# Queries, keys and values of the stick-breaking and undilated heads kept in DRAM, and sixteen seven-product pairs per layer

## The chip, the cores and the metric

The kernel runs on one core of a Trainium2 chip. The core has a matrix engine (TensorE, PE in the profile), a vector engine (VectorE, DVE), an engine for activations and copies (ScalarE, ACT), a general one (GpSimd, POOL) and SyncE (SP), which here issues nearly all DMA transfers. Each engine takes its own instructions in order. The metric is the device time of one execution in microseconds; less is better.

## The reference, cut to what matters

Two layers over 1024 tokens of width 1024, all in float32. Per layer:

```python
h = rmsnorm(x, norm1[l])
qa, ka, va, qb, kb, vb, gate_pre = split(h @ w_in[l])
o_a = dilated_mixture(qa, ka, va)            # 12 heads of 64: 4 undilated, 4 with dilation 4, 4 with 16
o_b = stick_breaking_attention(qb, kb, vb)   # 4 heads of 64
g_a, g_b = split(sigmoid(gate_pre + b_gate[l]))
x = x + (g_a * (o_a @ w_br[:256]) + g_b * (o_b @ w_br[256:])) @ w_o[l]
a, v = split(rmsnorm(x, norm2[l]) @ w_up[l])
x = x + (gelu(causal_conv(a)) * v) @ w_down[l]
```

and a last rmsnorm. The undilated heads see a window of 128 keys, the dilated ones every 4th or 16th key. Stick-breaking weighs key s for query t by `sigmoid(z_ts)` times the product of `1 - sigmoid(z_tj)` over all j between s and t.

## The kernel before, in words

Every float32 operand is split in two parts of a shorter type, `hi` and `lo` (`split`, L132: a ScalarE cast and a VectorE subtraction), and a product is three matmuls: hi by hi, hi by lo, lo by hi. A **plain** product of 128 columns of weights with 512 tokens is 8 x 3 matmuls of 128x512 (`product`, L167). A **seven-product pair** (`pair`, L1012) computes two such blocks of columns over all 1024 tokens as a 2 by 2 block product with seven instead of eight block products. It needs sums of blocks of `h` (`block_sums`, L951, kept as `t_hi`, `t_lo`; POOL, VectorE and ScalarE make them from `h_sum`) and sums of blocks of the weights, made anew for every pair on POOL and VectorE.

The mixer of a layer (`mixer`, L1169) runs in this order. `head` (L581) makes the stick-breaking values and the first two heads' keys and queries. Then `attend` (L328) walks a list of attention items: 16 of stick-breaking (`stick_item`, four heads by four blocks of 256 queries), 4 undilated or near ones (`near_item`, one per head), 16 dilated or far ones (`far_item`, which serve both dilations). An item has score steps and, per block of keys, a `turn` (transposes) and an `apply` (products with the values). After each such step `Dense.advance` (L301) adds the item's rate to an account and issues that many steps of **dense work** from a list: a step is six 512-wide matmuls, or their like. TensorE's order is exactly the order in which this Python is written out (`manual_schedule` for PE); the other engines and SP are ordered by a planner, by priority and by when its model thinks an instruction is ready.

Dense work before: `dense.main` holds the second stick-breaking pair's keys and queries, the undilated values and the two undilated pairs' keys and queries as plain units, and six seven-product pairs for the dilated heads; `dense.plain` holds 8 plain gates (`PLAIN`), `dense.seven` 4 gate pairs. `choose` (L225) takes seven-product pairs from `main` only when no plain gate is left. `until` (L309) issues dense steps until a name is done; `aside` (L245) issues one piece of the block sums at a time. What an attention item waits for by name (`first` in `attend`) is a count of dense steps, not a semaphore: `LEAD` is the number of steps between the order of a fetch and the name that lets the item in.

Keys, queries and values of the dilated heads go to DRAM (`tk`, `tv`) with tokens regrouped and come back per item (`fetch_kq`, L800; `fetch_v`, L805). Those of the stick-breaking and undilated heads stay in SBUF (`R["kb"]`, `R["qb"]`, `R["vb"]` and so on). When an item list ends, `join` (L905) merges the dilated and the undilated outputs with factors made by `factors` (L880), and the branch products `br_ps` follow.

Buffers go by tags with a fixed number of slots: `xa` has 4 (values, the fetched keys and queries, the near output `on`, later x), `e8` has 6 (keys, queries, `stay`, and the block sums), `ql` 2 (the low parts of queries, then the raw weights of a pair), `ps`, `s`, `t`, `o` 2 PSUM banks each.

Of the kernel before, what the change touches and what calls it, by code (L numbers as in the profile page):

```python
# [12 lines left out]
ALU = mybir.AluOpType  # L13
# [29 lines left out]
RATE = (0.68, 0.85, 0.72, 0.62)  # L43
RATE_B = (0.9, 1.6, 0.75, 1.1, 0.65, 0.9, 0.6, 0.3)
PLAIN = 8
# [12 lines left out]
def trunk_kernel(ctx, tc, x, norm1, w_in, b_gate, w_br, w_o, norm2, w_up, conv_w, conv_b, w_down, norm_f, out, depth=None, probe=None):  # L58
# [57 lines left out]
    tv = [dr.tile([2, 4, P, 2, 256], F32, name=f"tv{i}") for i in range(2)]  # L116
    dn = [dr.tile([4, T], F32, name=f"dn{i}") for i in range(2)]
# [14 lines left out]
    def split(hi, lo, src, turn=None):  # L132


        one = act.copy(hi, src)  # L135
        if turn == "is":
            LAST["act"] = one.ins.name
        elif turn == "waits" and LAST:
            tc.add_manual_dep(one.ins, LAST["act"], NO_SYNC, reason="in turn")
        two = dve.tensor_tensor(lo, src, f32(hi), ALU.subtract)  # L140
        if turn == "is":
            LAST["dve"] = two.ins.name
        return two
# [68 lines left out]
    class Dense:  # L212
# [4 lines left out]
        def __init__(self):  # L217
# [5 lines left out]
            self.scored = self.applied = self.kq = self.v = 0  # L223

# [24 lines left out]
        def fetch(self):  # L249
# [4 lines left out]

            while self.kq < self.scored + 2 and there(self.kq):
# [72 lines left out]
    def attend(dense, items):  # L328
# [4 lines left out]
        for i, (name, first, rest, rate, make) in enumerate(items):  # L333
# [37 lines left out]
            for j, f in enumerate(seq):  # L371
                if nxt and j >= at:
# [133 lines left out]
    def new_v(name):  # L506
        return [sb.tile([P, 4, 4, P], F32R, tag="xa", bufs=4, name=name) for _ in range(2)]

    def values(key, l, off):
        w = weights(w_in[l][:, off : off + 256], 256)  # L510
        yield
        vt = R[key] = new_v(key)
        yield from values_part(vt, w, range(4))

    def values_part(vt, w, ms):
        for m in ms:
# [15 lines left out]
            dve.tensor_tensor(vv[:, :, :, 64:128], ov, f32(vv[:, :, :, 0:64]), ALU.subtract)  # L532
            yield


    def keys_half(kt, w, n):
        o = bank("ps", "k_ps")
        yield from product(o, [(w[k], h_part(n, k)) for k in range(KD)])
        ka, kb = (kt[:, i, n * HF : (n + 1) * HF] for i in range(2))
        act.copy(ka[0:64], o[0:64])  # L540
        act.copy(kb[64:128], o[64:128])
        dve.tensor_tensor(ka[64:128], o[0:64], f32(ka[0:64]), ALU.subtract)
        dve.tensor_tensor(kb[0:64], o[64:128], f32(kb[64:128]), ALU.subtract)
        yield

    def queries_half(q, w, n, scale):
        qt, ql = q
        o = bank("ps", "q_ps")
        yield from product(o, [(w[k], h_part(n, k)) for k in range(KD)])
        qa, qb, la, lb = (a[:, i, n * HF : (n + 1) * HF] for a in (qt, ql) for i in range(2))  # L550
        for q2, src in ((qa, o[0:64]), (qb, o[64:128])):
            act.mul(q2[0:64], src, scale)
            act.mul(q2[64:128], src, scale)
        dve.scalar_tensor_tensor(la[0:64], o[0:64], scale, f32(qa[0:64]), ALU.mult, ALU.subtract)
        dve.scalar_tensor_tensor(lb[64:128], o[64:128], scale, f32(qb[64:128]), ALU.mult, ALU.subtract)
        yield

    def new_q():


        qt, ql = big("qt", F32R), sb.tile([P, 2, T], F32R, tag="ql", bufs=2, name="ql")
        for rows, i in ((slice(64, 128), 0), (slice(0, 64), 1)):
            zeros_ = pool.memset(f32(ql[rows, i, :]), 0.0)
            tc.add_manual_dep(zeros_.ins, LAST["pool"], NO_SYNC, reason="in turn")
        return qt, ql

    def keys(key, l, off):
        w = weights(w_in[l][:, off : off + P], P)
        yield
        kt = R[key] = big("kt", F32R)  # L570
        for n in range(2):
            yield from keys_half(kt, w, n)

    def queries(key, l, off, scale):
        w = weights(w_in[l][:, off : off + P], P)
        yield
        q = R[key] = new_q()
        for n in range(2):
            yield from queries_half(q, w, n, scale)

    def head(l):  # L581
# [11 lines left out]
        vt = R["vb"] = new_v("vb")  # L593
        kt = R["kb", 0] = big("kt", F32R)
        if l:
            q = R["qb", 0] = new_q()
            yield from values_part(vt, wv, range(2))
        else:
            yield from values_part(vt, wv, range(1))
            wk, wq = others()  # L600
            q = R["qb", 0] = new_q()
            yield from values_part(vt, wv, range(1, 2))
        for n in range(2):
            yield from keys_half(kt, wk, n)
            yield from queries_half(q, wq, n, SCALE)
# [27 lines left out]
    def stick_item(pr, s, qp):  # L633
        if "ob" not in R:
            R["ob"] = big("ob")
        q, k, vt, ob = R["qb", pr], R["kb", pr], R["vb"], R["ob"]
        hd = 2 * pr + s
        rows, st, shared = {}, {}, {}

        def score(a):  # L640
# [3 lines left out]
            if a == 0:  # L644
                st[0] = big("stay")
            sv = st[0][:, a, :]
            for c0 in range(0, L, 512):
                w = min(512, L - c0)
                z = bank("s", "z")
                scores(z[:, :w], *(t[:, s, i * P : i * P + P] for t in q), k[:, s, c0 : c0 + w])  # L650
# [6 lines left out]
            for c1 in range(L, 0, -512):  # L657
                SCANS.append((bt, sv, max(0, c1 - 512), c1, L, pr == 1 and qp == 2 and s == 0))
            if L <= 512:
                scans()  # L660

# [27 lines left out]
        def apply(kb):  # L689
# [4 lines left out]
            for j in range(2):  # L694
                c = P if last and j else 0
                for p in (0, 1):
                    pe.matmul(
                        o[:, c:256],
                        vt[(kb + j) // 4][:, (kb + j) % 4, hd, :],
# [4 lines left out]
                    )  # L704
            if last:
                fold(ob[64 * s : 64 * s + 64, pr, qp * 256 : (qp + 1) * 256], o)
                if (pr, s, qp) == (1, 1, 3):
                    nc.sync.dma_start(obd, ob)
# [5 lines left out]
    def near_item(pr, s):  # L714
# [1319 lines left out]
```

## Time and profile before

| | us |
|---|---|
| median of the runs | 2662.72 (2661.96 to 2663.26, 3 runs) |
| span of the profiled execution | 2660.2 |
| TensorE busy in it | 2647.5 |
| VectorE busy | 2036.5 |
| ScalarE busy | 1349.6 |
| POOL busy | 647.1 |

The median is 2.5 us above the span; the span runs from the first to the last instruction. The granted TensorE clock is full throughout. The first layer's mixer lies at 0 to some 600 us, its feed-forward part up to 1310, the second layer behind it. In rows of instruction groups the columns are line, engine, operation, output and inputs with shapes, count, then busy time and mean nanoseconds of one, then the engine's idle time ahead of them and what ended it. In rows of a timeline they are start and duration in microseconds. In rows of a stretch they are the stretch, its length, then busy time and count of each engine (PE, PEld, DVE, ACT, POOL), the granted clock, the DMA engines' busy share and GB/s. In rows of waits they are the sum, the number and the longest. In rows of one tile the three numbers are the shortest, median and longest duration in nanoseconds. In rows of DMA issues they are the count, the size of one and the median time to landing.

### The profile page before, as it was taken

The page shows a single profiled execution, that of the slowest core. Times are in us where ns is not written, and L with a number is a line of the kernel's source. Part 1 is how long each engine was busy: PE and PEld are TensorE (multiplying, and loading weights), DVE is VectorE, ACT ScalarE, POOL GpSimd, SP SyncE. Part 2 cuts the span into 40 slices and gives each one's busy share as a digit, 9 for nine tenths or more (in the row PEclk, how much of TensorE's full clock was granted, in tenths as well). Part 3 has the DMA queues.
Part 4 walks back from the last instruction along what each step waited for, and adds up shares of the span by engine and source line. Part 5 has one row for each costly group of instructions (what it writes and reads, how often), then busy time and mean ns, then how long its engine had stood idle before and what let it go on. Part 6 is the DMA issues. An engine that isn't in the chain of part 4 may idle for free.

```text
span 2660.2 us, 36616 instructions
## 1 busy us (share of the span) xinstructions
PE 2647.5 (100%) x13084; PEld 2227.1 (84%) x13084; DVE 2036.5 (77%) x3087; ACT 1349.6 (51%) x2490; POOL 647.1 (24%) x473
## 2 busy tenths in 40 slices
PE   9999999999999999999999999999999999999999
PEld 8988888888888888888889888888888888888888
DVE  5877856685888888897658777566958888898865
ACT  6556645474545555432445565455645455554225
POOL 2003211121233344321210051110321343343200
PEclk9999999999999999999999999999999999999999
DMA  5212178673243544688411122785632544446963
GB/s 183 63 53 84 50 196 246 203 263 102 76 150 138 172 143 158 231 310 321 151 40 40 48 84 85 200 263 182 240 97 71 179 138 153 148 168 246 341 242 118
DMA packets 360195, 424.19 MB, mean 159 GB/s; under 512 B 20693, under 2 KB 289357, under 8 KB 357965
## 3 DMA queue, kind: packets, MB, share of 16 engines
q1 hardware_dynamic: 359996, 421.85, 47.8%
q8 instruction: 103, 1.69, 0.3%
q14 instruction: 80, 0.65, 0.1%
q10 hardware_dynamic: 16, 0.00, 0.0%
HBM read 278.07 MB, written 143.72 MB: 159 GB/s over the span
## 4 chain that ended last, share of the span: by engine, by line
PE 91%; DVE 6%; issue 1%; ACT 1%; DMA 1%; POOL 0%; SPq 0%; DVEq 0%; ACTq 0%
PE u_a L945 5%; PE u_a L947 5%; PE u_a L946 5%; PE d_ps L1662 5%; PE d_ps L1664 4%; PE d_ps L1663 4%; PE i_a L945 3%; PE u_c L945 3%; PE u_c L947 3%; PE u_c L946 3%; PE i_a L947 3%; PE i_a L946 3%; PE o_ps L172 2%; PE o_ps L174 2%; PE o_ps L173 2%; PE g_ps L172 2%
## 5 line engine op out<-in xcount | busy, mean ns | idle before, releaser
L140 DVE TENSOR_TENSOR w_lo<-up_a,w_hi 128x512 fp32r<-128x512 f32 x240 | 237.6, 997 | 20.5 <-ACT w_hi L135 20.5
L135 ACT CAST w_hi<-up_a 128x512 fp32r<-128x512 f32 x240 | 149.4, 622 | 183.6 <-PE u_a L946 49.5
L1670 DVE TENSOR_TENSOR x<-x,d_ps 128x512 f32<-128x512 f32 (+1 forms) x228 | 152.0, 672 | 76.8 <-PE d_ps L1664 75.6
L1401 POOL TENSOR_TENSOR cv<-cv 128x512 f32<-128x512 f32 x88 | 132.3, 1515 | 249.3 <-DVE cv L1396 139.4
L140 DVE TENSOR_TENSOR g<-cv,g 128x512 fp32r<-128x512 f32 x154 | 152.1, 988 | 5.2 <-ACT g L135 2.7
L140 DVE TENSOR_TENSOR w_lo<-w_raw,w_hi 128x512 fp32r<-128x512 f32 x144 | 106.4, 741 | 54.9 <-ACT w_hi L135 54.5
L135 ACT CAST w_hi<-w_raw 128x512 fp32r<-128x512 f32 x144 | 89.2, 621 | 105.0 <-PE o_ps L173 50.4
L135 ACT CAST w_hi<-in_a 128x512 fp32r<-128x512 f32 x120 | 74.4, 620 | 114.3 <-PE i_a L946 41.9
L1662 PE MATMUL d_ps<-gd_in,w_hi 128*128 128x512 f32 (+1 forms) x340 | 130.3, 383 | 1.4 <-ACT w_hi L135 0.6
L1664 PE MATMUL d_ps<-gd_in,w_lo 128*128 128x512 f32 (+1 forms) x340 | 129.8, 382 | 0.0
L1663 PE MATMUL d_ps<-gd_in,w_hi 128*128 128x512 f32 (+1 forms) x340 | 129.7, 382 | 0.0
L140 DVE TENSOR_TENSOR w_lo<-in_a,w_hi 128x512 fp32r<-128x512 f32 x120 | 88.6, 738 | 51.0 <-ACT w_hi L135 49.4
L945 PE MATMUL u_a<-hh,w_hi 128*128 128x512 f32 x320 | 124.7, 390 | 0.8 <-DVE u L1552 0.8
L946 PE MATMUL u_a<-hl,w_hi 128*128 128x512 f32 x320 | 124.5, 389 | 0.0
L947 PE MATMUL u_a<-hh,w_lo 128*128 128x512 f32 x320 | 124.5, 389 | 0.0
L947 PE MATMUL u_a<-t_hi,w_lo 128*128 128x512 f32 x320 | 124.5, 389 | 0.0
L945 PE MATMUL u_a<-t_hi,w_hi 128*128 128x512 f32 x320 | 124.5, 389 | 0.0
L946 PE MATMUL u_a<-t_lo,w_hi 128*128 128x512 f32 x320 | 124.5, 389 | 0.0
L1034 POOL TENSOR_TENSOR u<-in_a 128x512 f32<-128x512 f32 x20 | 28.8, 1439 | 369.5 <-DMA in_a<-in_w_in_dram 142.5
L135 ACT CAST g<-cv 128x512 fp32r<-128x512 f32 x154 | 94.9, 617 | 41.2 <-POOL cv L1401 30.0
L669 DVE TENSOR_TENSOR_SCAN stay<-stay,zero 128x512 f32<-128x512 f32 (+2 forms) x96 | 93.5, 974 | 28.0 <-ACT stay L655 27.4
L1662 PE MATMUL d_ps<-gd_in,wd 128*128 128x512 f32 (+1 forms) x292 | 113.9, 390 | 0.0
(412 smaller groups left out, 8694.2 us busy)
## 6 DMA issues: line engine op xcount, KB each, us to landing
gd<-g SPq DMA_DIRECT2D x154, 512.0 KB, 3.5
gd_in<-gd SPq DMA_DIRECT2D x154, 512.0 KB, 5.9
up_a<-in_w_up_dram SPq DMA_DIRECT2D x80, 512.0 KB, 5.3
t_kq<-tk SPq DMA_DIRECT2D x32, 768.0 KB, 5.6
wd_raw<-in_w_down_dram SPq DMA_DIRECT2D x22, 1024.0 KB, 12.6
w_raw<-in_w_in_dram SPq DMA_DIRECT2D x80, 256.0 KB, 3.0
in_a<-in_w_in_dram SPq DMA_DIRECT2D x40, 512.0 KB, 4.7
gin<-gs SPq DMA_DIRECT2D x32, 512.0 KB, 4.7
```

The costliest lines, as they stand in the source:

```text
L135: one = act.copy(hi, src)
L140: two = dve.tensor_tensor(lo, src, f32(hi), ALU.subtract)
L172: pe.matmul(o, lh, rh, start=(first and i == 0), stop=False, skip_group_check=share)
L669: one = dve.tensor_tensor_scan(rev, rev, zero[:, 0:1].to_broadcast([P, c1 - c0]), 1.0 if c1 == L else sv[:, c1 : c1 + 1], ALU.mult, ALU.add)
L945: pe.matmul(o, w[0][:, c], rh, start=(first and i == 0), stop=False, skip_group_check=True)
L946: pe.matmul(o, w[0][:, c], rl, start=False, stop=False, skip_group_check=True)
L947: pe.matmul(o, w[1][:, c], rh, start=False, stop=(last and i == 3), skip_group_check=True)
L1401: return lambda: pool.tensor_tensor(dst, a, b, ALU.subtract)
L1662: pe.matmul(o[:, sub], wh[:, c], gh[:, sub], start=(i == 0 and k in (0, 4, 5)), stop=False, skip_group_check=True)
L1663: pe.matmul(o[:, sub], wh[:, c], gl[:, sub], start=False, stop=False, skip_group_check=True)
L1664: pe.matmul(o[:, sub], wl[:, c], gh[:, sub], start=False, stop=(i == m - 1), skip_group_check=True)
L1670: dve.tensor_tensor(x, x, o[:, sub], ALU.add)
```

## The change

Five things are done together.

- Queries, keys and values of the stick-breaking and undilated heads are written to DRAM, a tensor per head (`sk`, `sq`, `sv`), and read back: a stick-breaking head in four rows of 256 tokens (`fetch_row`), a near head whole (`fetch_whole`). The low part of the queries is padded with zeros, which `zeros` now writes once, ahead of everything in layer 0, together with those of `tk`.
- The plain units for these heads become pairs: `pair_near` for keys and queries, `pair_v` with g = 0 for the undilated values. With `PLAIN` 4 instead of 8 two more gate pairs come. A layer has 16 seven-product pairs and 4 plain gates.
- The block sums no longer wait for named items; they start with the layer's last head units and go on with the first attention head.
- Stick-breaking runs head after head, four rows each, instead of two heads in turn. All rates are new.
- `attend` tries at every step whether the next item may begin.

```diff
-RATE = (0.68, 0.85, 0.72, 0.62)
-RATE_B = (0.9, 1.6, 0.75, 1.1, 0.65, 0.9, 0.6, 0.3)
-PLAIN = 8
+RATE = (1.0, 1.2, 1.35, 1.4)
+RATE_N = 0.85
+RATE_T = 0.8
+PLAIN = 4
...
+    sk = [dr.tile([P, T], F32, name=f"sk{i}") for i in range(8)]
+    sq = [dr.tile([P, 2, T], F32, name=f"sq{i}") for i in range(8)]
+    sv = [dr.tile([P, KD, P], F32, name=f"sv{i}") for i in range(8)]
...
+            def row(j):
+                u, qp = divmod(j, 4)
+                return j < 16 and {f"K{u}", f"V{u}"} <= self.done and (u == 0 or (self.rows >= 4 * u and self.free[qp] >= u))
+
+            def whole(v):
+                return v < 4 and self.b == 16 and self.rows == 16 and {f"K{4 + v}", f"V{4 + v}"} <= self.done and self.near >= v
+
+            while row(self.b):
+                fetch_row(self.b)
+                self.at(LEAD, lambda j=self.b: self.done.add(f"FB{j}"))
+                self.b += 1
+            while whole(self.n):
+                fetch_whole(self.n)
+                self.at(LEAD, lambda v=self.n: self.done.add(f"FN{v}"))
+                self.n += 1
...
             for j, f in enumerate(seq):
+                if pending:
+                    begin()
+                    gap, at = max(1.0, (len(seq) - j) * 0.5 / max(1, len(nxt))), j
...
+    def keep_kq(c, n, u, hi, lo):
+
+        t = slice(n * HF, (n + 1) * HF)
+        for s in range(2):
+            rows = slice(64 * s, 64 * s + 64)
+            if c:
+                for src, kind, up in ((hi, 0, 0), (hi, 0, 64), (lo, 1, 0)):
+                    nc.sync.dma_start(sq[u + s][up : up + 64, kind, t], f32(src[rows]))
+            else:
+                for src, up in ((hi, 0), (lo, 64)):
+                    nc.sync.dma_start(sk[u + s][up : up + 64, t], f32(src[rows]))
...
+    def fetch_row(j):
+
+        u, qp = divmod(j, 4)
+        if j == 0:
+            R["kv"] = sb.tile([P, 2, T], F32R, tag="xa", bufs=4, name="kv")
+        if "slots" not in R:
+            R["slots"] = sb.tile([P, 4, 2, 256], F32R, tag="xa", bufs=4, name="slots")
+        t = slice(256 * qp, 256 * qp + 256)
+        nc.sync.dma_start(f32(R["kv"][:, 0, t]), sk[u][:, t])
+        nc.sync.dma_start(f32(R["slots"][:, j % 4]), sq[u][:, :, t])
+        nc.sync.dma_start(f32(R["kv"][:, 1, t]).rearrange("p (b c) -> p b c", c=P), sv[u][:, 2 * qp : 2 * qp + 2, :])
+
+    def fetch_whole(v):
+        kv = R["kvn", v] = sb.tile([P, 2, T], F32R, tag="xa", bufs=4, name="kv")
+        nc.sync.dma_start(f32(kv[:, 0, :]), sk[4 + v])
+        for k in range(2):
+            nc.sync.dma_start(f32(R["slots"][:, :, k, :]), sq[4 + v][:, k, :].rearrange("p (m c) -> p m c", c=256))
+        nc.sync.dma_start(f32(kv[:, 1, :]).rearrange("p (b c) -> p b c", c=P), sv[4 + v])
...
-                st[0] = big("stay")
+                st[0] = sb.tile([P, 2, T], F32, tag="xa", bufs=4, name="stay")
...
-        series({"B17"}, 3, lambda i: first(3, b22, b12, i), 6, 4)
-        series({"N01s"}, 1, lambda i: first(1, b12, b11, i), 6, 4)
+        series(set(), 3, lambda i: first(3, b22, b12, i), 4, 3)
+        series(set(), 1, lambda i: first(1, b12, b11, i), 4, 3)
         for i in range(4):
-            todo.append(({"N01s"}, lambda i=i: less(b22, i)))
-        series({"N11s"}, 2, lambda i: i or new_s(2), 0, 1)
+            todo.append((set(), lambda i=i: less(b22, i)))
+        series(set(), 2, lambda i: i or new_s(2), 0, 1)
...
     def zeros():
         none = sb.tile([P, 4, 256], F32, tag="ot", name="none")
-        one = pool.memset(none[0:64], 0.0)
-        tc.add_manual_dep(one.ins, LAST["pool"], NO_SYNC, reason="in turn")
+        pool.memset(none[0:64], 0.0)
+        for u in range(8):
+            nc.sync.dma_start(sq[u][64:128, 1, :], none[0:64].rearrange("p a b -> p (a b)"))
...
+    def pair_near(dense, l, u):
+
+
+        offs = (OFF_KA + 64 * u - 256, OFF_QA + 64 * u - 256) if u > 3 else (OFF_KB + 64 * u, OFF_QB + 64 * u)
...
         else:
+            zeros()
             first_units = relay(head(l))
...
         dense.main = [
...
+            *((None, set(), f, True) for f in (pair_near(dense, l, 2), pair_v(dense, l, 0), pair_near(dense, l, 4), pair_near(dense, l, 6))),
+            *((None, set(), f, True) for f in (pair_v(dense, l, 1), pair_kq(dense, l, 1, 0), pair_kq(dense, l, 2, 0))),
+            *((None, set(), f, True) for f in (pair_v(dense, l, 2), pair_kq(dense, l, 1, 1), pair_kq(dense, l, 2, 1))),
         ]
         items = []
+        for j in range(16):
+            items.append((f"B{j // 4}{j % 4}", [f"FB{j}"], [], RATE[j % 4], lambda j=j: stick_item(dense, j // 4, j % 4)))
+        for v in range(4):
+            items.append((f"N{v // 2}{v % 2}", [f"FN{v}"], [], RATE_N, lambda v=v: near_item(dense, v // 2, v % 2)))
```

More of the change, by code (lines that the diff above doesn't have):

```diff
@@ L558, in new_q @@
[L558 to L572, printed above, removed]
```

170 lines of the change are left out of this document (75 added, 95 removed).

## The prediction

> **What bounds the kernel now.** I read the page's busy shares and its chain first, then the waits of TensorE, then TensorE's timeline, then the busy time by stretch.
>
> ```profile
> span 2660.2 us, 36616 instructions
> PE 2647.5 (100%) x13084; PEld 2227.1 (84%) x13084; DVE 2036.5 (77%) x3087; ACT 1349.6 (51%) x2490; POOL 647.1 (24%) x473
> PE 91%; DVE 6%; issue 1%; ACT 1%; DMA 1%; POOL 0%; SPq 0%; DVEq 0%; ACTq 0%
> PE warm L1926 <- POOL ident masks.py:199: 1.6, 1, 1.6
> PE u_ps L173 <- DVE hl L499: 1.3, 2, 0.7
> PE sb_t L685 <- DVE beta L673: 0.5, 2, 0.2
> 1000.09 0.39 PE L945 MATMUL u_b<-hh,w_hi 128*128 128x512 f32 x1
> 1002.81 0.39 PE L945 MATMUL u_a<-hh,w_hi 128*128 128x512 f32 x1
> 102.58 0.28 PE L172 MATMUL v_ps<-w_hi,hh 128*128 128x256 f32 x1
> 103.53 0.28 PE L174 MATMUL v_ps<-w_hi,hl 128*128 128x256 f32 x1
> 555.35 1.04 PE L916 MATMUL j_ps<-ident,fx 128*128 128x128 f32 x8
> 556.14 0.48 PE L945 MATMUL i_a<-hh,w_hi 128*128 128x512 f32 x1
> 540.00:600.00 60.00, 60.00 (x294) 50.36 (x293) 56.13 (x91) 44.11 (x80) 18.96 (x16) 1.00 0.82 285
> ```
>
> TensorE is busy from end to end and its largest wait is 1.6 us, at the start. So time is the number of matmuls times their pitch, and a matmul taken out is gained only if no wait takes its place. A mean duration (390 ns) overlaps the next matmul; the pitch is from start to start. Twelve 512-wide matmuls lie between 1000.09 and 1002.81: 0.2267 us each. Eight 256-wide ones lie between 102.58 and 103.53: 0.119 us. Eight transposes take 555.35 to 556.14: 0.099 us. In the last row VectorE is busy 56.13 of 60 us and TensorE still 60.00, so VectorE can run at 94% without holding TensorE up.
>
> **The change part by part.**
>
> *Fewer matmuls.* A plain pair of 128-column products over 1024 tokens is 2x2x8x3 = 96 matmuls, a seven-product pair 7x4x3 = 84. Per layer five such pairs change (keys and queries of the second stick-breaking pair, those of the two undilated pairs, two gate pairs): 5 x 12 x 0.2267 = 13.6 us. The undilated values were 192 matmuls at 0.119 = 22.8 us; as a pair they cost 84 x 0.2267 = 19.0 and 16 transposes at 0.099 = 1.6: 2.2 us less. Two layers: **31.7 us off TensorE**. Scores, transposes and products of the heads stay.
>
> *The dense work runs out.* A step of dense work is six matmuls. A pair gives 14 steps, a plain gate 8: 16 x 14 + 4 x 8 = 256 per layer (before: 268). The rates ask for: 6 + 2 steps before the first item; per stick-breaking head 4x1.0 + 6x1.2 + 8x1.35 + 10x1.4 = 36, four heads 144; four near items at 14 x 0.85, 47.6; again 6 + 2 before the first far item; then 5 x 0.8 = 4 per far item. 256 - 208 leaves 48, which is 12 of the 16 far items. The last four are left without cover, and so is what follows them. Before, pairs went on to the end: dense matmuls lie on both sides of the last spread transposes at 555.35.
>
> ```profile
> L845 ACT ACTIVATE p<-p,st 128x256 f32<-128x256 f32 x64 | 39.5, 617 | 29.1 <-DVE st L844 28.3
> L845 ACT ACTIVATION_READ_ACCUMULATOR p<-p,st 128x1 f32 x64 | 12.0, 187 | 0.0
> L135 ACT CAST p1h<-t 128x384 fp32r<-128x384 f32 x64 | 30.0, 479 | 21.5 <-PE t L854 21.2
> L140 DVE TENSOR_TENSOR p1l<-t,p1h 128x384 fp32r<-128x384 f32 x64 | 35.0, 556 | 29.5 <-ACT p1h L135 28.9 <-DMA tk<-kq_l 0.6
> 541.60 0.22 PE L612 MATMUL z<-t_kq 128*128 128x128 f32 x1
> 542.52 0.27 PE L852 MATMUL t<-ident,p 128*128 128x128 f32 x1
> 552.12 0.28 PE L862 MATMUL o<-p1h,t_v 128*128 128x256 f32 x1
> 552.54 0.44 PE L945 MATMUL i_b<-hh,w_hi 128*128 128x512 f32 x1
> t_kq<-tk SPq DMA_DIRECT2D x32, 768.0 KB, 5.6
> 548.04 2.75 POOL L902 COPY fx<-sf 128x512 f32<-128x512 f32 x4 [39.63 <-DVE sf L895]
> ```
>
> A far item on TensorE is a score (541.60 to 542.52, 0.9), two turns of three transposes (0.3 each) and two applies (552.12 to 552.54, 0.4 each): 2.3 us. On ScalarE it is 2 x 617 + 2 x 187 + 2 x 479 ns and half a fold, near 2.8 us. Two key buffers are left, and each waits for a score before its 5.6 us fetch: (5.6 + 0.9)/2 = 3.2 us per item. So an uncovered item takes 3.2, not 2.3: 0.9 x 4 = 3.6 us. After the last score comes a chain with nothing under it: exponentials, two turn-cast-subtract-apply rounds, then the factors, whose copies on POOL alone took 2.75 us before the spread transposes can start. I put 3.4 us on that: **7 us per layer, 14 in all**. Bounds: 3 per layer (ScalarE's 0.5 x 4 and one late apply, 0.479 + 0.556) and 13 (no overlap between items).
>
> *Heads from DRAM.* Writes and reads of Q, K, V add some 30 MB per layer. A stick-breaking row is three small fetches ordered six steps (8 us) ahead; the copies of equal size in the next fence land in 3 to 5. I cost them at nothing; their cover is the dense step. A near head is a 2 MB fetch, four times the 512 KB of one gate load:
>
> ```profile
> gin<-gs SPq DMA_DIRECT2D x32, 512.0 KB, 4.7
> w_raw<-in_w_in_dram SPq DMA_DIRECT2D x80, 256.0 KB, 3.0
> 0.00:10.00 10.00, 7.76 (x39) 6.94 (x40) 5.31 (x15) 5.89 (x10) 2.62 (x15) 1.00 0.83 291
> 10.00:20.00 10.00, 10.00 (x84) 9.30 (x83) 6.04 (x13) 9.68 (x23) 6.14 (x6) 1.00 0.75 236
> 20.00:30.00 10.00, 10.00 (x83) 9.73 (x82) 7.11 (x22) 7.89 (x18) 4.83 (x5) 1.00 1.04 341
> L1010 SPq DMA_DIRECT2D tk<-none x8: 610/1192/1235, 66.1 to 73.1; - x8
> ```
>
> At 236 to 341 GB/s it takes 6 to 9 us, ordered six steps and some attention work ahead (10 us): just enough, if its buffer is free. The tag `xa` has four buffers, and near heads need the slots, the output and up to three key-value tiles: the fourth head's tile waits until the second head's last apply, two steps before its scores, so some of a 4.7 us load shows. SP waits there too, and the weights of later pairs queue behind it, with a pair's time to spare. I take 2 us per layer, **4**; bounds 0 (copies of Q ahead of K) and 10 (three heads exposed).
>
> *Zeros at the start.* 16 copies, 4 MB, move to the front or are new there. SP needs about 1.2 us for each of the old eight and, by the shorter form of 0.6, 5 us for the new: up to 14 us of queue that the token loads stand behind, and 4 MB at 341 GB/s is 12 us of engines already at 0.75 to 1.04. But the first loads are issued before the zeros are made, and later ones wait for buffers. **3 us**, bounds 0 and 12 (no gain: TensorE has no wait where they stood, at 66 to 73). The memset of `ql` goes; it was off the path.
>
> *VectorE, and the block sums.*
>
> ```profile
> L669 DVE TENSOR_TENSOR_SCAN stay<-stay,zero 128x512 f32<-128x512 f32 (+2 forms) x96 | 93.5, 974 | 28.0 <-ACT stay L655 27.4
> L673 DVE TENSOR_TENSOR beta<-beta,stay 128x512 f32<-128x512 f32 (+2 forms) x96 | 53.2, 556 | 2.5
> L140 DVE TENSOR_TENSOR sbl<-sb_t,sbh 128x512 fp32r<-128x512 f32 (+1 forms) x80 | 50.5, 633 | 16.2 <-ACT sbh L135 15.9
> L140 DVE TENSOR_TENSOR w_lo<-in_a,w_hi 128x512 fp32r<-128x512 f32 x120 | 88.6, 738 | 51.0 <-ACT w_hi L135 49.4 <-PE t L749 1.6
> L140 DVE TENSOR_TENSOR w_lo<-up_a,w_hi 128x512 fp32r<-128x512 f32 x240 | 237.6, 997 | 20.5 <-ACT w_hi L135 20.5
> L965 POOL TENSOR_TENSOR h_sum<-h_sum,hh x16: 1284/1297/1657, 241.4 to 1594.2; 128x512 f32<-128x512 f32 x16
> L976 DVE TENSOR_TENSOR h_sum<-hh,h_sum x16: 676/682/1668, 280.1 to 1639.4; 128x512 f32<-128x512 f32 x16
> ```
>
> Scans, products and casts of eight heads are 93.5 + 53.2 + 50.5 = 197 us, with masks and folds some 229: 28.6 per head. A pair asks VectorE for 7 x 0.738 and nine operations near 0.69: 11.4 us. A head covered by 36/14 pairs needs 28.6 + 29.3 = 58 us while TensorE has 36 x 6 x 0.2267 + 116 x 0.12 = 63: 92%. The first head has the sums instead, 32 operations near 0.8: 60 of 63. That is the share that 540 to 600 carries without a wait, but the scan chain is longer: **3 us** in all, bounds 0 (TensorE's waits for VectorE are under 3 us in sum, so nothing is to be gained) and 14.
>
> The row L976 spreads from 676 to 1668 and POOL's from 1284 to 1657: both stretch when they meet. The Trainium skill ("SBUF — State Buffer", section "SBUF: two separate sides") says why: an exclusive lock, where a VectorE operation with two SBUF inputs and a GpSimd operation that reads SBUF block each other for a whole instruction. The trace agrees (997 against 738 ns for one cast where POOL is busier). By that rule 24 sums on POOL could each hold VectorE 1.3 us, 31 us per layer in the first head, and the forecast would turn into a loss; it is the page's voice for the second rival.
>
> *The rest.* Fewer and wider casts in the layer's first units, 16 small writes for one of `ob`, another interleaving into layer 1: all beside matmuls, nothing.
>
> Sum: 31.7 - 14 - 4 - 3 - 3 = 7.7 us less. Against the profiled 2660.2, 2652.5; the median of the runs, 2662.72, stands 2.5 above that span: **2655**.
>
> **The rivals.**
>
> *All of the gain.* The far items' tail is hidden, because the weights of the branches and the casts of `ob` are then prepared early. For it: the sums' buffers come free sooner. Against: TensorE's order is written out. 2662.7 - 31.7 + 4 = 2635.
>
> *VectorE becomes the bound of the stick-breaking heads* (the other side). If casts cost 997 instead of 738 and sums double, a head needs 58 + 36/14 x 7 x 0.26 = 63: the point from which every microsecond more is TensorE's. Three more per head, eight heads, is 24: 2679. Against: 540 to 600.
>
> *Nothing left.* The tail at 10 per layer instead of 7 and the start at 5: 2655 + 8 = 2663.
>
> **How the numbers follow.** A kernel of this length can be told from no change beyond 0.2%, 5.3 us. My sum 0.40 (2645 to 2657), all of it 0.12, nothing left 0.18, VectorE or near fetches as the bound 0.30. Faster 0.52, same 0.18, slower 0.30. The range leaves one in ten on either side: 2633 (all of it) to 2684 (the second rival, with the near fetches' 10); the sum's own is 2645 to 2665.
>
> **What would show it.** Right: 84 matmuls for each pair and no `v_ps` 256-wide ones in the attention; waits of transposes and `o` on ScalarE, VectorE and `t_kq` in the last four far items; few waits before. Wrong: waits of `sb_t` on `beta`, of near scores on DMA, or of `x_t` on `xr`, above a microsecond each; or dense matmuls up to the spread transposes.

## The result and the profile after

The changed kernel takes 2786.37 us (median of 4 runs, 2783.34 to 2787.56) against 2662.34 for the kernel before on the same chip: **slower, by a ratio of 1.0464, 95% interval [1.0449, 1.0479]**, 124 us. The prediction was 2655, with a range to 2684. It was wrong in sign and size.

The page of the kernel after, first its span, then busy time and count of each engine:

```profile
span 2784.3 us, 36703 instructions
PE 2658.9 (95%) x12780; PEld 2211.2 (79%) x12780; DVE 2082.1 (75%) x3151; ACT 1343.6 (48%) x2488; POOL 675.7 (24%) x481
```

TensorE issues 304 matmuls fewer (13084 before), but it no longer fills the span. The ten largest sums of waits of TensorE in the kernel after (sum, number, longest), where before the largest was 1.6 us:

```profile
PE warm L1967 <- DMA g_raw<-in_norm_dram: 25.7, 1, 25.7
PE sb_t L705 <- DVE beta L693: 17.7, 14, 3.2
PE nrm_t L506 <- DVE nrm L459: 11.9, 2, 11.8
PE z L613 <- DMA kv<-sk: 9.5, 2, 5.2
PE z L613 <- DVE vv L1153: 7.3, 6, 2.0
PE kq_ps L176 <- DVE vb L550: 5.8, 1, 5.8
PE kq_ps L177 <- POOL hl L523: 5.5, 2, 4.7
PE v_t L1149 <- DVE u L1088: 5.2, 4, 2.4
PE v_ps L176 <- DVE kq_l L572: 5.0, 1, 5.0
PE j_ps L939 <- POOL fx L925: 4.3, 2, 2.2
```

To place the loss I summed, over all matmuls of each trace, the time from one start to the next beyond the pitch of its width (0.227, 0.174, 0.1195 and 0.109 us for 512, 384, 256 and 128 columns). I call this the excess. It is 26.8 us before and 181.8 after: 155.0 more. Less the 31.7 of matmuls removed that makes 123.3; the spans differ by 124.1. (The two sums must agree, since the excess is the span less the pitches; what the account adds is the place of the loss.) By stage, both layers together, in us (the feed-forward parts differ by less than 1):

| stage | excess before | after | more |
|---|---|---|---|
| start and the layers' first units | 6.1 | 72.3 | 66.2 |
| stick-breaking heads | 5.0 | 53.0 | 48.0 |
| near heads | 5.2 | 17.5 | 12.3 |
| far items and branch products | 4.1 | 33.0 | 28.9 |

Busy time by stretch in the kernel after: the start, the first layer's units, the same place of the second layer, and the first layer's stick-breaking heads.

```profile
0.00:20.00 20.00, 1.65 (x6) 1.36 (x6) 0.00 (x0) 0.00 (x0) 3.43 (x16) 1.00 0.86 199
60.00:80.00 20.00, 15.00 (x93) 13.45 (x93) 13.03 (x29) 7.13 (x13) 16.48 (x12) 0.94 0.56 163
80.00:100.00 20.00, 14.18 (x66) 12.59 (x64) 15.17 (x15) 3.87 (x7) 14.96 (x10) 0.72 0.47 131
1400.00:1420.00 20.00, 10.01 (x66) 8.94 (x64) 12.70 (x11) 4.44 (x8) 18.83 (x13) 0.81 0.08 24
118.00:402.00 284.00, 266.84 (x1337) 219.11 (x1336) 218.40 (x362) 154.70 (x315) 30.74 (x20) 0.99 0.55 152
```

TensorE does 1.65 us of work in the first 20 (the kernel before had 17.76 us there). From 60 to 100 and from 1400 POOL, the fifth pair of numbers, is busy 15 to 19 of 20 us: these are the block sums, which stand in the layer's first units, although the program names them at their end and with the first head. With no condition left on them the planner takes them early; the run with sums held tests this. SP's timeline at the start, and ScalarE's first load:

```profile
0.74 0.39 SPq L1880 DMA_DIRECT2D xr<-in_x_dram  x1
1.95 8.87 SPq L1030 DMA_DIRECT2D sq<-none  x8
10.86 9.99 SPq L1034 DMA_DIRECT2D tk<-none  x8
20.90 2.40 SPq L1883 DMA_DIRECT2D w_raw<-in_w_in_dram  x2
23.34 0.55 SPq L1880 DMA_DIRECT2D xr<-in_x_dram  x1
24.58 0.58 ACTq L1869 DMA_DIRECT2D g_raw<-in_norm_dram  x1
```

After one load of x come the 16 zero writes, 18.9 us of SP's queue, and only then the weights and the other tokens: the first weights go out at 20.90 us, 19.7 later than before (1.20). The wait of 25.7 us itself ends with another load, the 4 KB of `g_raw`. ScalarE issues it, not SP, and it goes out at 24.58 us instead of 0.74: `g_raw` has the buffer tag `ot`, of which there is one buffer, and `zeros` now takes that buffer first, for `none`. So this load waits until the zero writes have landed. Both delays come from the place of `zeros`, and no run takes them apart; the weights alone, by their 19.7 us, would have held up the first products for most of that time.

### The profile page after: what moved, and what is told of

Same layout as the page of the kernel before. It is cut to its first block, busy times and chain, and to the rows that moved or that the text cites. A ratio compares the mean times of both kernels' runs of the same rounds, so it can differ in the third digit from the quotient of the medians.

```text
span 2784.3 us, 36703 instructions
## 1 busy us (share of the span) xinstructions
PE 2658.9 (95%) x12780; PEld 2211.2 (79%) x12780; DVE 2082.1 (75%) x3151; ACT 1343.6 (48%) x2488; POOL 675.7 (24%) x481
## 3 DMA queue, kind: packets, MB, share of 16 engines
q8 instruction: 101, 1.65, 0.3%
## 5 line engine op out<-in xcount | busy, mean ns | idle before, releaser
L1058 POOL TENSOR_TENSOR u<-in_a 128x512 f32<-128x512 f32 x32 | 45.2, 1411 | 818.3 <-DMA in_a<-in_w_in_dram 275.8
L139 ACT CAST w_hi<-in_a 128x512 fp32r<-128x512 f32 x192 | 119.1, 620 | 150.2 <-PE i_a L969 50.4
L144 DVE TENSOR_TENSOR w_lo<-in_a,w_hi 128x512 fp32r<-128x512 f32 x192 | 139.2, 725 | 45.6 <-ACT w_hi L139 45.3
L144 DVE TENSOR_TENSOR w_lo<-w_raw,w_hi 128x512 fp32r<-128x512 f32 x96 | 71.0, 742 | 62.1 <-ACT w_hi L139 61.6
L1691 PE MATMUL d_ps<-gd_in,wd 128*128 128x512 f32 (+1 forms) x292 | 113.9, 390 | 0.0
L1693 PE MATMUL d_ps<-gd_in,wd 128*128 128x512 f32 (+1 forms) x292 | 112.8, 386 | 0.0
L1692 PE MATMUL d_ps<-gd_in,wd 128*128 128x512 f32 (+1 forms) x292 | 112.8, 386 | 0.0
```

Of the source, the lines that this page charges most:

```text
L1058: pool.tensor_tensor(u2, a11, a21, ALU.subtract)
L1691: pe.matmul(o[:, sub], wh[:, c], gh[:, sub], start=(i == 0 and k in (0, 4, 5)), stop=False, skip_group_check=True)
L1692: pe.matmul(o[:, sub], wh[:, c], gl[:, sub], start=False, stop=False, skip_group_check=True)
L1693: pe.matmul(o[:, sub], wl[:, c], gh[:, sub], start=False, stop=(i == m - 1), skip_group_check=True)
```

## The experiments

Theory A: two moves in the order of issue, the zeros and the unheld sums, cost the time ahead of attention; four smaller causes follow in attention (VectorE beside POOL, the transposes of the pairs' values, the near fetch, the far tail). Rival B: VectorE is the bound of the heads, and whatever is moved costs the same elsewhere. Each ratio below is to the kernel before. The intervals of zeros late, zeros spread, the near fetch, eight gates and dense work held back touch or overlap those of the run that they are compared with; there the stages of the trace say more than the time.

**Zeros late.**

```diff
-            zeros()
             first_units = relay(head(l))
...
+            zeros()
             for _ in first_units:
```

> One part undone: the zeros of the query spaces are written after the first loads of x, at the end of the first layer's start, instead of ahead of them; the rest is the changed kernel (2786 us). Theory A (moves in the order of issue cost the time): in the changed kernel the SP queue holds the 16 zero writes for 19 us (0.98 to 20.9 us) ahead of the first weight and x loads, and TensorE's first real work waits 25.7 us; so the time falls by 20 to 26 us, to about 2762. Rival (what was lost at the start is covered later, or the writes only move their collision to the first head's fetches): 2780 to 2786.

2778.84 us (1.0436 [1.0419, 1.0453]): 7.5 less, not 24. The wait at the start is gone, and another is there, as the rival said:

```profile
PE z L613 <- DMA slots<-sq: 19.2, 1, 19.2
```

**Sums held.**

```diff
         in_parts(c, SCALE, hi, lo, o)
+        R["gate"] = lo[:, 0:1]
...
+            if "last" not in keep:
+                keep["last"] = pool.tensor_copy(r[:, 0:1], f32(R["gate"])).ins.name
             one = pool.tensor_tensor(r, f32(al), f32(bl), ALU.subtract)
```

The last values tile sets the gate too, and the head's units issue no sums.

> The other part undone: the block sums of h are held until the layer's first values, keys and queries are done, by one small GpSimd copy of the last of these tiles ahead of the first sum; nothing else changes (2786 us before). Theory A: the sums, free to run as soon as h is there, fill GpSimd and slow VectorE in the layer's first units, where TensorE loses 21 us in the first layer beside the zeros and 28 us in the second against its own pitch; held, about 40 us come back: about 2745. Rival B (the sums cost the same wherever they run, because VectorE is what bounds the first heads): the loss moves into the first stick-breaking head and at most 15 us come back: 2771 or more.

2770.97 us (1.0402 [1.0386, 1.0417]): 15.4 less. The second layer's first units are clean (0.7 us of excess, 25.4 in the kernel after), but its stick-breaking heads went from 26.6 to 46.0.

**Both.**

> The zeros late and the sums held together. Theory A, with the two independent of each other: 2786 - 24 - 40 = about 2722, still above the kernel before (2662), since the stick-breaking heads (24 us a layer), the fourth undilated head (6 us) and the far tail (14 us a layer) keep their losses. Rival B: 2745 or more, with the stick-breaking heads longer than 283 us a layer.

2755.76 us (1.0344 [1.0329, 1.0359]), 30.6 less. More than the two alone, less than theory A said, and the stick-breaking heads are longer (288.7 and 298.9 us from the first score to the last transpose, against 283.1 and 283.4 in the kernel after), as rival B said. The first layer's part has its own reason, in SP's timeline of this run and TensorE's waits from 60 to 100:

```profile
66.00 8.37 SPq L1035 DMA_DIRECT2D sq<-none  x8
74.42 9.86 SPq L1039 DMA_DIRECT2D tk<-none  x8
89.35 2.58 SPq L645 DMA_DIRECT2D slots<-sq  x4
```

```profile
PE z L615 <- DMA slots<-sq: 17.8, 1, 17.8
```

The block of zeros takes 18.2 us of SP's queue here too, and the first head's queries stand behind it. Late zeros had only moved the block. Whether SP or the transfers set its length stays open: from 66 to 84 us the DMA engines are 95% busy, and spread out, as in the next run, the eight writes to `sq` take SP 0.60 us in the median instead of 1.05 on the mean.

**Zeros spread.** Two writes at that place, the other 14 one by one between the sums.

```diff
+        for f in todo[:2]:
+            f()
+        return todo[2:]
```

> As the kernel with zeros late and sums held (2755.8 us; there SP issued the 16 zero writes in a row from 66.0 to 84.3 us, and the first scores waited 17.8 us for the queries queued behind them), but only the two zero writes that the first two heads read stay there, and the other 14 go out one by one between the block sums. Theory (the zeros cost what SP's queue needs to issue them, 18 us, wherever they stand in one block ahead of something awaited): 2755.8 - 17 = about 2739. Rival (the 4 MB themselves fill the DMA engines, 90% busy in these 100 us, and delay the fetches from wherever they are): 2750 or more.

2744.10 us (1.0308 [1.0285, 1.0332]), 11.7 less; the first layer up to its first scores has 5.8 us of excess, as before the change (5.3), and the first scores wait 0.2 us for their queries instead of 17.8. Start and first units are settled. The time is 42.3 us less than with the whole change, not the 66.2 of the table, because the heads, where the sums now stand, have 78.7 us of excess instead of 53.0.

**Rates.**

```diff
-RATE = (1.0, 1.2, 1.35, 1.4)
+RATE = (1.6, 1.8, 1.3, 0.9)
```

> As the kernel with spread zeros, and the steps of dense work per attention step in a stick-breaking head are 1.6, 1.8, 1.3, 0.9 for its four blocks of queries, instead of 1.0, 1.2, 1.35, 1.4; the sum over a head stays at 36. In the trace with late zeros and held sums the waits of TensorE for beta and stay are at the second and third blocks, and the fourth has 0.2 to 2.4 us of excess in 20. Theory C (a wait for latency: the next block's scans take longer than the dense work given to cover them): 15 to 25 us come back in the two layers. Rival B (VectorE, 79% busy, is the bound of these heads): within 5 us of the kernel with spread zeros.

2765.36 us (1.0383 [1.0367, 1.0398]): 21 slower, which neither side expected. The plain gates are used up sooner, and the sums not yet made are then, by the program, all issued ahead of the first pair: the first head's fourth block loses 17.4 and 16.8 us (6.4 and 2.4 with spread zeros). Two waits of this run, of which the 10.0 stands in that block:

```profile
PE sb_t L707 <- DVE beta L695: 29.7, 12, 10.0
PE i_a L971 <- DVE t_lo L144: 5.8, 3, 3.0
```

In the other three heads of the first layer the loss mostly moved from the third block to the second: 7.0, 7.3 and 6.1 us a head became 6.0, 7.0 and 5.6.

**No sums.**

```diff
-        series(set(), 3, lambda i: first(3, b22, b12, i), 4, 3)
...
+            for t, f in ((3, b22), (1, b12), (2, b11), (4, b21)):
+                S[t] = f()
```

> As the kernel with spread zeros, with the block sums of h left out: the seven-product pairs read blocks of h in their place, so what they compute is left wrong, with the same products and the same instructions outside the sums. It gives the price of the sums where they now stand. Theory D (VectorE and GpSimd work of the sums delays the first head's scans): in the first head's second and third blocks the excess of 6.7 us (first layer) and 11.2 us (second) goes, and 10 to 18 us come back in all. Rival (the excess is the same in the heads without sums, 4 to 8 us each, and belongs to the order of work): under 5 us come back.

2708.48 us (1.0169 [1.0152, 1.0186]): the sums, with the casts and subtractions of their results, cost 35.6 us, twice the most that was expected. The stick-breaking heads' excess falls from 38.4 and 40.3 to 21.4 and 21.9 in the two layers, in the first head from 18.0 and 18.7 to 2.0 and 1.4.

**Near fetch gated.**

```diff
-... <= self.done and self.near >= v
+... <= self.done and self.near >= v and (v < 2 or f"N0{v - 2}" in self.done)
```

> As the kernel with spread zeros, with one condition more on the fetch of the third and fourth near heads: it is issued, and its six steps are counted, only once the head two before has made its last product, so that its buffer is free. Theory (the wait of 4.5 us and 2.9 us of the scores for the fourth head's keys is the wait of the fetch for that buffer, with no dense work put between): 5 to 8 us come back in the two layers, and the wait for the DMA goes. Rival (the transfer itself is late, or the dense work taken there is missed later): within 3 us of the kernel with spread zeros.

2736.86 us (1.0278 [1.0263, 1.0294]), 7.2 less. The wait for `kv<-sk` is gone, the near heads' excess is 1.0 a layer (4.8 and 6.0 with spread zeros). That much is shown; the gain in time is not clear of the spread of the runs. In the two traces the stick-breaking heads, which the edit doesn't touch, differ by as much the other way (78.7 and 87.4 us).

**Sums on VectorE.** Timelines of VectorE and then of POOL in the run with the gated fetch, first head (start, duration):

```profile
83.92 1.17 DVE L695 TENSOR_TENSOR beta<-beta,stay 128x127 f32<-128x127 f32 x1
85.01 1.75 DVE L691 TENSOR_TENSOR_SCAN stay<-stay,zero 128x256 f32<-128x256 f32 x1
86.68 0.27 DVE L673 TENSOR_TENSOR z<-z,mask_b 128x128 f32<-128x128 f32 x1
```

```profile
83.68 1.26 POOL L993 TENSOR_TENSOR h_sum<-h_sum,hh 128x512 f32<-128x512 f32 x1
84.90 1.31 POOL L989 TENSOR_TENSOR h_sum<-hl,hl 128x512 f32<-128x512 f32 x1
86.29 1.53 POOL L992 TENSOR_TENSOR h_sum<-h_sum,hh 128x512 f32<-128x512 f32 x1
```

The `beta` of 127 columns takes 1.17 us and ends at 85.09, when POOL's operation at 83.68 has ended (84.94) and the next has begun; the mask, which reads `z` in PSUM, takes its 0.27 beside the sum. In the trace with spread zeros the five of these `beta` that have no POOL operation beside them take 0.29 on the mean. The edit, on the kernel with the gated fetch:

```diff
-            one = pool.tensor_tensor(r, f32(al), f32(bl), ALU.subtract)
+            one = dve.tensor_tensor(r, f32(al), f32(bl), ALU.subtract)
...
-            pool.tensor_tensor(r, r, f32(ah), ALU.add)
+            dve.tensor_tensor(r, r, f32(ah), ALU.add)
```

> As the kernel with spread zeros and the gated near fetch (2736.9 us), with the 24 sums of a layer that GpSimd makes moved to VectorE; the same sums, the same order. In the trace with spread zeros a VectorE operation of two SBUF operands beside one of these sums takes 1.68 instead of 0.68 us (in_a) and 1.24 instead of 0.69 (beta), one with a PSUM operand does not change (0.29 and 0.29, 0.68 and 0.67). Theory D1 (the sums cost time because GpSimd holds VectorE up, about 1 us each; on VectorE they take 0.7): 24 x (1.0 to 1.3 - 0.7) = 7 to 14 us of VectorE a layer less, and 8 to 20 us come back. Rival D2 (what costs is the length of the chain of the sums and the order of work, not the engine): within 5 us. Rival D3 (VectorE bounds these heads by its own work): 16 us of VectorE more a layer, 10 to 30 us slower.

2720.03 us (1.0217 [1.0199, 1.0236]), 16.8 less although VectorE has more to do. Thirty us of the first head, with the sums on POOL and then on VectorE:

```profile
78.00:108.00 30.00, 23.35 (x100) 18.14 (x100) 24.56 (x28) 12.80 (x28) 24.79 (x17) 0.89 0.67 177
```

```profile
78.00:108.00 30.00, 26.74 (x131) 21.32 (x130) 29.50 (x55) 16.52 (x36) 0.00 (x0) 1.00 0.78 210
```

VectorE finishes 55 operations instead of 28, TensorE 131 matmuls instead of 100. But VectorE is now busy 29.50 of 30 us: here, in the first head, it is the bound by its own work.

**Transposes of the values in other banks,** and two steps later, on the kernel with the gated fetch.

```diff
-            tp = bank("s", "v_t")
+            tp = bank("t", "v_t")
...
-            dense.at(2, lambda: turn(c, n, f))
+            dense.at(4, lambda: turn(c, n, f))
```

> As the kernel with the gated near fetch (2736.9 us), with the transposes of the values pairs in the banks of the attention's transposes instead of those of the scores, and made four steps after the pair's product instead of two. In its trace the scores wait 8.0 us for vv, the transposes of v 7.0 us for u. Theory F (these are waits for a bank and for a sum that two steps don't cover): 8 to 15 us come back. Rival (VectorE is late by as much wherever it is asked): within 4 us, the waits stand at sb_t instead.

2721.42 us (1.0227 [1.0211, 1.0243]), 15.4 less. TensorE's waits in the run with the gated fetch alone, then in this one:

```profile
PE z L615 <- DVE vv L1163: 8.0, 7, 2.3
PE v_t L1159 <- DVE u L1098: 5.4, 4, 2.4
```

```profile
PE sb_t L707 <- DVE beta L695: 24.3, 17, 2.8
PE sb_t L707 <- DVE vv L1163: 4.3, 6, 1.5
```

The transposes' own waits are gone, the scores no longer wait for `vv`, the other transposes wait 4.3 for it. Bank and place were changed together; what each brings alone was not run.

**A filler for the tail.** One more gate product at the end of each layer's dense work, on the kernel with the gated fetch. The added products don't leave the gate's values as they were, contrary to the text below, so the run counts for its time alone.

```diff
+            if self.extra and self.started:
+                return [None, self.extra.pop(0), False, 0]
```

> As the kernel with the gated near fetch (2736.9 us), with one unneeded gate product more at the end of each layer's dense work (its 48 products of 0.227 us, 10.9 us a layer, write the same values a second time; no rate is changed). Far items and branch lose 16 us a layer there. Theory E (these waits are latency that nothing covers, since dense work is spent): the added products fall into them, far and branch keep their length within 3 us a layer, and the time rises by 2 to 8 us to about 2742. Rival (the items wait on something that the products do not cover, or VectorE is the bound): the whole 21.8 us are added, 2755 or more.

2757.94 us (1.0360 [1.0341, 1.0379]), 21.1 slower: the added 21.8 in full. Dense work ends in the fifteenth far item instead of the thirteenth, but the last dense matmul and the first transposes of the joining still stand far apart:

```profile
586.26 0.39 PE L178 MATMUL g_ps<-hh,w_lo 128*128 128x512 f32 x1
599.33 1.12 PE L944 MATMUL j_ps<-ident,fx 128*128 128x128 f32 x4 [1.35 <-POOL fx L930]
```

So filling the items between moves the bare end, it doesn't cover it. An earlier try was a lower rate beside the far items alone, on the kernel with zeros late and sums held (it also lets the fetches go on when dense work is spent):

> As the kernel with zeros late and sums held, and the rate of dense work beside the dilated far items 0.58 steps instead of 0.8, so that it lasts to the sixteenth item rather than to the twelfth. Theory (the tail of the far items is uncovered because dense work is spent): far plus branch lose 17 us a layer against 2 before, so 10 to 14 us a layer come back, 20 to 28 in all: about 2698. Rival (the far items are slow because the branch product and the factors wait on VectorE and GpSimd, whatever lies beside them): within 6 us of the kernel without the new rate.

2766.13 us (1.0388 [1.0372, 1.0403]), 10.4 slower than without; its first far stage has 17.3 us of excess instead of 13.7. This run did not do what it was made for. By TensorE's order its dense work ends in the eleventh far item, two earlier than without: two items together now take 54 dense matmuls instead of 48, since each second item first issues the steps that are counted until its fetch's name is done. It says nothing on whether cover would help.

**Eight plain gates,** as before the change.

```diff
-PLAIN = 4
+PLAIN = 8
```

> As the kernel with the gated near fetch (2736.9 us), with one part of the change undone: eight plain gate products ahead of the pairs instead of four (14 pairs a layer instead of 16). TensorE's own work grows by 2 pairs x 2 layers x 12 x 0.227 = 10.9 us. Theory G (fewer products are worth less than their pitch, since the attention's waits lie open and the added products cover them, and the sums get more time before the first pair): the time falls by 5 us or more in spite of them. Rival (products cost their pitch): 2748.

2743.78 us (1.0306 [1.0290, 1.0323]): 6.9 slower for 10.9 us of added products (against the gated fetch), between the two. In the traces the stick-breaking heads lose 19.0 us less, as theory G said, and the near and far stages 12.4 more. What a product taken out brings can't be read more closely from this time.

**All together, and with dense work held back.** All is zeros spread, sums held and on VectorE, the fetch gated, the transposes moved.

> Zeros spread, sums held and on VectorE, the near fetch gated, the transposes of the values in the other banks: all that was measured to help, together. If the four causes are separate, 2736.9 - 16.8 (sums on VectorE) - 15.4 (transposes) = 2704.7. If the sums and the transposes delay the same chain (VectorE's scans), less: 2712 or more.

2703.73 us (1.0160 [1.0144, 1.0175]), as added up: the sums on VectorE and the moved transposes gain 33.1 us together, 16.8 and 15.4 alone.

```diff
-RATE = (1.0, 1.2, 1.35, 1.4)
-RATE_N = 0.85
-RATE_T = 0.8
+RATE = (1.0, 1.2, 1.35, 1.2)
+RATE_N = 0.75
+RATE_T = 0.7
```

> As the kernel with all of these, with dense work held back for the end: 1.2 steps instead of 1.4 beside the fourth block of a stick-breaking head, 0.75 instead of 0.85 beside the near items, 0.7 instead of 0.8 beside the far ones. By the order of the program, dense work then reaches the sixteenth far item, where it ended at the thirteenth before; the run with 0.58 for the far items alone did not reach it, and the added gate product moved the end without filling the last two items. Theory E (the last three items, the joining and the branch's first products wait for latency, and only dense work that stands beside them covers it): far and branch fall by 8 to 14 us a layer, what is taken from the fourth blocks costs 0 to 4 us a layer, so 8 to 24 us come back in all. Rival H (dense work covers latency in equal measure wherever it stands, so taking it elsewhere loses what the tail gains): within 6 us of the kernel with all.

2696.93 us (1.0129 [1.0114, 1.0144]), 6.8 less (here too fetches go on when dense work is spent). Dense work now reaches into the sixteenth far item, close to the joining (last dense matmul, first spread transposes):

```profile
569.57 0.54 PE L973 MATMUL i_a<-hh,w_lo 128*128 128x512 f32 x1
573.87 1.50 PE L942 MATMUL j_ps<-ident,fx 128*128 128x128 f32 x12
```

Far items and branch gained 2 to 3.5 us a layer, the stick-breaking heads, with less beside their fourth blocks, 2 to 3 as well. So lack of cover is a part of the tail's loss, and 14 to 15 us a layer stay there that this cover doesn't take away. About half of them are waits that the trace names, in both layers together: `o` for `p1h` and `p1l` 5.1 us, `br_ps` for its weights and for the joined outputs 5.0, `j_ps` 3.6, `t` for `on` 1.6. No run takes them away, so their cause stays open.

**All without the sums.**

> The block sums left out again (the seven-product pairs read blocks of h in their place, so what they compute is left wrong), with spread zeros, the gated fetch and the transposes in the other banks. It bounds what no placing of the sums can bring. 2708.5 (without sums, spread zeros) - 7 (gated fetch) - 15 (transposes) = about 2686; against the kernel with all it gives the price of the sums on VectorE, 10 to 20 us for both layers. Rival (without the sums VectorE has room, and the transposes' waits hide): 2695 or more.

2684.74 us (1.0084 [1.0067, 1.0101]): as added up. The sums on VectorE still cost 19.0 us. And without them the kernel is 23 us above the one before, with 31.7 us fewer matmuls: the stick-breaking heads' 14 to 17 us a layer and the end's 17 to 19 remain. No version tried beats the kernel before.

## Why the prediction was wrong, point by point

- **31.7 us off TensorE.** Right: 120 matmuls of the five pairs and 184 of the values make the 304 missing. The conclusion from it, that cover is there for the rest, was not.
- **Zeros at the start, 3 us.** Wrong, and by the step "the first loads are issued before the zeros are made". Only one load is. The size of SP's work was near (up to 14 us predicted, 18.9 measured), but it was made a bound and then argued away. The start lost 25.7 us in one wait. That the zeros' buffer is also that of `g_raw` was not in the prediction at all. Taking the zeros back out of the start was worth little until they were also taken out of the way of the first head's queries: the same 4 MB, spread, hold up neither.
- **The rest, nothing.** The step that failed is "fewer and wider casts in the layer's first units ... another interleaving into layer 1: all beside matmuls". It looked at the units' own instructions and not at what lost its condition. The sums, free of their conditions, ran there; the first units of the second layer lost 24.6 us, and 0.7 us is left in all with the sums held.
- **VectorE and block sums, 3 us (bounds 0 to 14).** The sums alone cost 35.6 us where they were meant to stand (in the first head). The failed step is taking 540 to 600 as the share VectorE carries without a wait. There no chain of scans stood ahead of the transposes. The second rival, VectorE as the bound of the heads, was nearer: the waits of `sb_t` on `beta` are there, and its price of three us a head was too small, 6 a head on the mean. But in the kernel after the first head loses no more than the others (6.4, 5.1, 7.8 and 7.0 us in the first layer); VectorE as the bound by its own work shows only with the sums held and made on VectorE. Part of what the sums cost is the Trainium skill's rule ("SBUF — State Buffer", section "SBUF: two separate sides"): an operation of VectorE with two SBUF inputs and a GpSimd operation that reads SBUF shut each other out. The timelines and the 16.8 us of the sums on VectorE agree with it; the rule's 31 us a layer, quoted in the prediction, is more than the 18 a layer that the sums cost altogether. Some 8 us a layer were missed outright: the transposes of the values pairs stand in the scores' banks, beside heads that now share them, and two steps behind their product. What the heads still lose without sums and with the transposes moved, 14 to 17 us a layer against 2.5 before, was in no term, and its cause stays open.
- **The dense work runs out, 7 us a layer.** The mechanism was right in part: dense work was to cover twelve of the far items, and it ends in the thirteenth. In the kernel after the last dense matmul is at 605.53 and the joining begins at 623.97 (in the timeline below), with small waits for `p1l` between (3.1 us in both layers). The loss is 14.5 a layer with the branch, just past the upper bound of 13. That only dense work is missing there was not borne out: holding dense work back to there gave 2 to 3.5 us.

```profile
605.53 0.39 PE L970 MATMUL i_a<-hh,w_lo 128*128 128x512 f32 x1
623.97 3.69 PE L939 MATMUL j_ps<-ident,fx 128*128 128x128 f32 x16 [2.05 <-POOL fx L925]
```

- **Near fetch, 2 us a layer.** The mechanism was right: the fourth head's scores wait 5.2 us for a tile that waits for a buffer, and gating the fetch ends it. The term was mis-sized: 2 a layer predicted, 6.2 a layer more excess than before. With the gate the near stage has 1.0 a layer, less than before the change (2.6).
- **Stick-breaking row fetches, nothing.** Right as far as the waits show: none of the kernel after's larger ones names them.
- **The signs of being wrong.** Two of those that the prediction named came: `sb_t` waits up to 3.2 us on `beta`, and a near score 5.2 us on a DMA.

## What to carry to other kernels

When a condition is taken off a piece of work, ask where the planner will put it and not where the program names it; a data dependence holds it back. Count a queue's time for every issue that is moved, and look at what is awaited behind it, and at who gets its buffer next, at the new place as well as at the old one. An engine's share of busy time in one stage says nothing about a stage with a longer chain through that engine.

## What the runs showed of the hardware

After a wait of some microseconds TensorE can come back at half pace. The timeline after the near fetch's wait in the kernel after:

```profile
452.82 0.40 PE L970 MATMUL i_a<-t_hi,w_lo 128*128 128x512 f32 x1
458.40 0.48 PE L613 MATMUL z<-kv,slots 128*128 128x128 f32 x1 [5.18 <-DMA kv<-sk]
459.42 0.63 PE L968 MATMUL i_b<-hh,w_hi 128*128 128x512 f32 x1
459.84 0.63 PE L969 MATMUL i_b<-hl,w_hi 128*128 128x512 f32 x1
...
463.46 0.40 PE L970 MATMUL i_b<-hh,w_lo 128*128 128x512 f32 x1
463.69 0.40 PE L968 MATMUL i_b<-hh,w_hi 128*128 128x512 f32 x1
```

For some 5 us the 512-wide matmuls stand 0.427 us apart instead of 0.227, and the granted clock from 458 to 463 is 0.50. In the whole kernel after 47 matmuls stand at that pitch, 9.4 us, against 2 before; the prediction priced waits without it. The Trainium skill ("TensorE: Matmul & The Clock Gate", Part 1) says that the clock falls to half after an idle window of about 3.4 us. This trace agrees for the wait of 5.18 us. A shorter one does it too, in the run with dense work held back:

```profile
126.03 0.84 PE L708 MATMUL sb_t<-ident,beta 128*128 128x128 f32 x3 [2.42 <-DVE beta L696]
127.09 0.63 PE L177 MATMUL g_ps<-hl,w_hi 128*128 128x512 f32 x1
127.52 0.63 PE L178 MATMUL g_ps<-hh,w_lo 128*128 128x512 f32 x1
...
129.79 0.45 PE L971 MATMUL i_a<-hh,w_hi 128*128 128x512 f32 x1
```

The wait of 2.42 us is followed by some 3 us at half pace; 3.4 us without a matmul were not needed here. Nor does each wait of that length do it: in the run with zeros spread, one of 3.37 us (to 426.74) is followed by full pace at a granted clock of 1.00.
